# GpSimd issues the output projection's stores, norms come in one transfer, head sums are split sooner, x is added late to two rows

## The chip, the cores and the metric

The kernel runs on one core of a Trainium2 chip. The metric is device time in microseconds (us) of one execution. Before the change it is 1361.49 us, the median of three runs (1359.12 to 1362.36).

## The reference

A decoder layer in float32, one batch of 2048 positions, width 1024. The input x is RMS-normalised and projected to 6144 columns. These feed a gated short convolution of 8 heads of 128 and a linear recurrent unit (LRU) of 16 heads of 64. Each head's output is RMS-normalised, multiplied by its gain and a SiLU gate; the 2048 columns go through one output projection, x is added, and a last RMS norm follows.

```
xn = rms_norm(x, ln_g)
proj = xn @ w_in                                   # 1024 -> 6144
y_conv = headwise_rms_norm(short_conv(...), 8, conv_out_g) * silu(g_conv)
y_lru = headwise_rms_norm(rg_lru(...), 16, lru_out_g) * silu(g_lru)
h = x + concat([y_conv, y_lru]) @ w_out            # 2048 -> 1024
out = rms_norm(h, final_g)
```

## The kernel before

**Products.** A float32 product is made of three matmuls of rounded operands: each operand is split into a high half (ScalarE's cast) and a low half (a subtraction on VectorE, DVE, or GpSimd), and high x high, high x low and low x high are summed in PSUM. Blocks of 1024 x 1024 are multiplied with seven instead of eight products of halves. The tiles `th`, `tl` hold the split half that stays for many steps (the right side), `s` the split half of one step (high and low side by side).

**Steps.** A step makes the products for one pair of row blocks or columns. `steps` lists 48 steps of the input projection and then 16 of the output projection, ("o", ph, m): ph = 0 is the LRU half of the 2048 columns, ph = 1 the convolution half, and m names rows 2m and 2m + 1 of 16 blocks of 128 positions. A step has six to eight slots, and a slot is 12 matmuls of 128 x 512 on one bank (line 924). The first step of a ph "opens" new right-side tiles, which `Change` loads and splits (lines 492, 435, 163).

**The order** is written by hand. `at(n, f)` puts f n slots later; `tick()`, called once a slot, runs what is due. Each engine takes its instructions strictly in the order in which they are written, and SyncE (SP), which issues nearly all DMAs, too: a DMA that waits for an engine holds up all behind it.

**Left side of the output projection.** The gated outputs, not yet normalised, lie in DRAM (`yd`, stored at line 624), and the reciprocal roots of the heads' mean squares in `rsd`. `load_z` loads two row blocks of `yd` into `raw` (line 292) and the norms, broadcast over partitions, into `zr`, and multiplies them on DVE (line 163). For ph = 1 the norm of one head serves 128 partitions, one transfer (line 282). For ph = 0 heads are 64 wide, so a tile needs two norms, in two transfers of 64 partitions (line 285). Steps m = 0 and 1 of both ph are made during the input projection (`jobs`, the preparation): their `s` tiles are stored in `so` and only loaded later. Steps m = 2 to 7 of ph = 0 load their rows two steps ahead.

**Head norms.** `finish` multiplies by the gate, stores, squares; `head_sums` reduces the squares of each head group on DVE (line 609). After the last one `head_norms(1)` runs: one slot later the sums are split (`rt`: a cast, line 575, and a subtraction on DVE), three slots after that TensorE sums them over partitions (`norm_ps`, line 582), then a transpose, a root, a reciprocal (line 603) and twelve stores of eight partitions each into `rsd` (line 595). These norms serve the rows from m = 4 on.

**Rows of the output.** In ph = 0, `outp` loads x (line 847), adds the products and stores the partial sum to `od` (line 857); in ph = 1 it loads `od`, adds, takes the mean square on ScalarE (line 863), scales on DVE (line 868) and stores the finished row (line 872). All these DMAs are SP's. The last step ends with a shorter path of its own (lines 877 to 887).

Of the kernel before, what the change touches and what calls it, by code (L numbers as in the profile page):

```python
# [15 lines left out]
ALU = mybir.AluOpType  # L16

P = 128
D = 1024
# [4 lines left out]
KT = D // P  # L24
# [14 lines left out]
def hymba_kernel(ctx: ExitStack, tc: tile.TileContext, x, xt, w_in, par, lamc, w_gate, w_out, final_g, out):  # L39
    nc = tc.nc  # L40
# [103 lines left out]
    def at(slots, *fs):  # L144
        if slots == 0:
            for f in fs:
                f()
        else:
            due.append([slots, fs])
# [105 lines left out]
    steps = [(kind, 0, k) for k in range(KT) for kind in "lab"]  # L255
    steps += [(kind, 1, k) for kind, k in zip("lablab", (0, 1, 1, 1, 0, 0))]
    steps += [(kind, 1, k) for k in range(2, KT) for kind in "lab"]
    steps += [("o", ph, m) for ph in range(2) for m in range(KT)]
    cols = {"l": (GLX, GLG), "a": (GC, GX), "b": (GB, GG)}

    def set_of(n):
# [7 lines left out]
    def load_z(h, m, zr, wait):  # L269
        r = [piece("raw") for _ in range(4)]  # L270
        fs = []
        for i in range(2):
            c, b = divmod(2 * m + i, NB)
            assert normed[c // 2]
            rs_ = rsd[c // 2][c % 2]
            zz_, zq_ = [], []
            z2 = wt(("u", "r")[i], "zr") if zr else None

            def norms(dst, k0, n):
                dst = dst.rearrange("p (k t) -> p k t", k=n)  # L280
                if h == 1:
                    nc.sync.dma_start(dst, rs_[b:b + 1, k0:k0 + n, :].broadcast_to((P, n, P)))
                else:
                    for w in range(2):
                        nc.sync.dma_start(dst[w * 64:w * 64 + 64], rs_[b:b + 1, k0 + w * KT:k0 + w * KT + n, :]
                                          .broadcast_to((64, n, P)))

            for q in range(2):
                zz = r[2 * i + q].rearrange("p (k t) -> p k t", k=NB)
                zq = z2[:, q * C:(q + 1) * C] if zr else piece("zr")  # L290
                k0 = (1 - h) * KT + q * NB
                nc.sync.dma_start(zz, yd[c][b, :, k0:k0 + NB, :])
                if not zr:
                    norms(zq, k0, NB)
                elif q == 1:
                    norms(z2, (1 - h) * KT, KT)
                zq = zq.rearrange("p (k t) -> p k t", k=NB)
                fs.append(lambda zz=zz, zq=zq: tt(zz, zz, zq, ALU.mult))
        if wait is not None:
            for i in range(2):  # L300
                at(max(wait + i, 1), *fs[2 * i:2 * i + 2])
        return r, fs
# [19 lines left out]
    def hl_done(n):  # L322
        hlc[0] -= n
# [15 lines left out]

    def jobs():  # L340
        tjobs = [(t, j) for t in (2, 3) for j in range(NB)]
        for ph, m in ((0, 0), (0, 1), (1, 0), (1, 1)):
            (a11, a12, a21, a22), fs = load_z(ph, m, False, None)
            yield from (None,) * 4
            for f in fs[:2]:
                f()
            yield
            for f in fs[2:]:
                f()
            yield  # L350
            if m:
                x_ = aux("s3")
                tt(x_, a11, a21, ALU.subtract)
                tt(a21, a21, a22, ALU.add)
            b = {}

            def blocks():
                if tjobs:
                    b[0] = tjobs.pop(0)
                    b[1] = [piece("traw") for _ in range(4)]  # L360
                    for p, src in zip(b[1], w_blocks(*b[0])):
                        nc.sync.dma_start(p, src)

            def sums():
                if b:
                    b11, b12, b21, b22 = b[1]
                    tt(b11, b12, b11, ALU.subtract)
                    tt(b12, b22, b12, ALU.subtract)

            def more():  # L370
                if b:
                    b11, b12, b21, b22 = b[1]
                    tt(b22, b22, b11, ALU.subtract)
                    tt(b21, b21, b22, ALU.subtract)
                    to = td[b[0]]
                    at(1, lambda: [nc.sync.dma_start(to[n], v) for n, v in enumerate((b22, b11, b12, b21))])
                    b.clear()

            blocks()
            prev = None  # L380
            nothing = lambda: None
            if m:
                items = [(0, a11, lambda: tt(a11, a21, a11, ALU.subtract)), (3, x_, nothing), (2, a21, nothing),
                         (1, a11, nothing), (4, a12, lambda: tt(a12, a12, a11, ALU.subtract)),
                         (6, a22, nothing), (5, a12, nothing)]
            else:
                items = [(n, v, nothing) for n, v in enumerate((a12, a22, a11, a21))]
            for n, (i, v, after) in enumerate(items):
                if prev:
                    prev()  # L390
                    prev = None
                while not may():
                    yield
                t, = hl_tile("so")
                nc.scalar.copy(t[:, 0:C], v)

                def prev(t=t, i=i, v=v, after=after, dst=so[ph, m]):
                    tt(t[:, C:2 * C], v, t[:, 0:C].bitcast(F32), ALU.subtract)
                    after()
                    at(2, lambda: nc.sync.dma_start(  # L400
                        dst[i], t.bitcast(F32).rearrange("p (h c) -> p h c", h=2)))
                    at(3, lambda: hl_done(1))

                yield
            prev()
            made.add((ph, m))
            sums()
            yield
            more()
            yield  # L410
            yield
            blocks()
            yield from (None,) * 4
            sums()
            yield
            more()
            yield from (None,) * 2
# [149 lines left out]
    def head_norms(h):  # L567
        sm_ = sums[0]
        rt, = hl_tile("rt")
        rh, rl = rt[:, 0:C], rt[:, C:2 * C]  # L570
        at(6, lambda: hl_done(1))
        v = {}

        def split():
            nc.scalar.copy(rh, sm_)
            tt(rl, sm_, rh.bitcast(F32), ALU.subtract)

        def add():
            v["ps"] = pss.tile([P, C], F32, tag="s", name="norm_ps")[:NR, 0:KT * R]
            parts = [(n, q) for n in range(2) for q in (rh, rl)]  # L580
            for m, (n, q) in enumerate(parts):
                nc.tensor.matmul(v["ps"], sel[n], q[:, (1 - n) * KT * R:(2 - n) * KT * R],
                                 start=m == 0, stop=m == 3)

        def root():
            v["rs"] = aux("hn")[:NR, 0:KT * R]
            nc.vector.transpose(v["rs"], v["ps"])
            nc.scalar.activation(out=v["rs"], in_=v["rs"], func=AF.Sqrt, scale=inv_hd, bias=eps[:NR])

        def store():  # L590
            for w in range(3):
                k0 = (w + 1) % 3 * KT
                for q in range(4):
                    p0 = w * R + q * 8
                    nc.sync.dma_start(
                        rsd[h].rearrange("i b k t -> (i b) k t")[:, k0:k0 + KT, q * R:(q + 1) * R],
                        v["rs"][p0:p0 + 8].rearrange("p (k r) -> p k r", k=KT))
            normed[h] = True

        split()  # L600
        at(3, add)
        at(4, root)
        at(5, lambda: nc.vector.reciprocal(out=v["rs"], in_=v["rs"]))
        at(5, store)

    def head_sums(h, kt, y):
        if summed[0] == 0:
# [4 lines left out]
        summed[0] += 1  # L612
        if summed[0] == 2 * KT:
            summed[0] = 0
            at(1 if h else 7, lambda: head_norms(h))

    def finish(d0, h, kt, y, sil, gain):
        def f1():
# [191 lines left out]
    def conv_b(h, k):  # L810
        g = wt("o2", "gb", bufs=O2)

        def put(which, bank, other):
# [12 lines left out]
                combine(g[:, 0:C] if which == 21 else g[:, C:N2], bank, other)  # L826
            if which == 21:
                silu(g)
                finish(6, h, k, t, g, pt[:, CG + k:CG + k + 1])

        return put

# [4 lines left out]
    def outp(ph, m):  # L837
        ob = [wt("hl", "ob", bufs=HL) for _ in range(2)]
        xr, rest = {}, []
        if ph == 1 and m == 0:  # L840
            fg[0] = wt("t", "fg")
            nc.sync.dma_start(fg[0], final_g.rearrange("(o d) -> o d", o=1).broadcast_to((P, D)))

# [2 lines left out]
            xr[i] = wt("ig", "xr", bufs=IG) if i == 0 else wt("o2", "xr", bufs=O2)  # L846
            nc.sync.dma_start(xr[i], x[tb * P:(tb + 1) * P, :] if ph == 0 else od[tb])

        last = ph == 1 and m == KT - 1
        at(2 if last else 5, lambda: load(0))  # L850
        at(2 if last else 6, lambda: load(1))

        def fin(i):
            tb = 2 * m + i
            if ph == 0:
                at(1, lambda: tt(xr[i], xr[i], ob[i], ALU.add))
                at(3, lambda: nc.sync.dma_start(od[tb], xr[i]))
                return
            ss = small.tile([P, 2], F32, tag="ss", bufs=4, name="ss")
            rs = small.tile([P, 1], F32, tag="rs", bufs=4, name="rs")  # L860
# [8 lines left out]
                                               op0=ALU.mult, op1=ALU.mult)  # L869

            def f3():
                nc.sync.dma_start(out[tb * P:(tb + 1) * P, :], ob[i])

            if last and i == 1:
                for d in (1, 0):
# [419 lines left out]
```

## Time and profile before

| | us |
|---|---|
| median of three runs | 1361.49 |
| the profiled execution | 1361.65 |
| its span (first to last instruction) | 1359.8 |
| TensorE (PE) busy | 1301.9, 96% |
| DVE busy | 1032.5, 76% |
| ScalarE (ACT) busy | 748.4, 55% |
| GpSimd (POOL) busy | 226.2, 17% |
| SP's DMA queue, share of 16 engines | 77.1% |

The output projection runs from about 1025 us to the end. The profile's page has the busy times; its windows give, for a stretch of the span, the busy us and instruction count of each engine, the granted TensorE clock (1.00 is full), the share of the 16 DMA engines' time that packets took, and GB/s. The share can pass 1.00, since packets of one engine overlap. A row of the waits names who waited for whom, us in total, times, and the longest. A row of a timeline has start, duration, engine, line and names, and in brackets the idle time before it with what ended it.

### The profile page before, as it was taken

The numbers are of one execution on the slowest core, as the hardware profiler recorded it, in microseconds if no ns is written. First come the engines' busy times: TensorE is split into PE (matmuls) and PEld (weight loads), VectorE is DVE, ScalarE is ACT, GpSimd is POOL, SyncE is SP. The second block draws the span as 40 slices with busy tenths as digits, with TensorE's granted clock in tenths as the row PEclk, the third lists the DMA queues.
The fourth block names the chain that finished last, engine by engine and source line by source line (L and its number), as shares of the span: only waits on it lengthen the run. The fifth ranks groups of instructions, "written<-read, shape, count | busy, mean of one in ns | idle before, by whom it ended". The sixth has DMA issues, their size and how long they took to land.

```text
span 1359.8 us, 16618 instructions
## 1 busy us (share of the span) xinstructions
PE 1301.9 (96%) x5648; PEld 1058.6 (78%) x5648; DVE 1032.5 (76%) x1245; ACT 748.4 (55%) x1139; POOL 226.2 (17%) x160
## 2 busy tenths in 40 slices
PE   6989999999999999899999999999999799998997
PEld 5867877777878787777888888888878688887886
DVE  7778788789989897978566676667458776759885
ACT  7475757575665757565544645364456233444443
POOL 3204242333334340101010110101000000000000
PEclk9989999999999999999999999999999899999999
DMA  7137797988879888542789999999778889797643
GB/s 284 31 119 258 270 252 273 278 296 302 319 281 330 291 291 304 173 162 79 247 304 286 335 354 331 332 339 365 228 253 313 249 236 227 271 404 260 240 146 136
DMA packets 158805, 355.28 MB, mean 261 GB/s; under 512 B 17920, under 2 KB 52736, under 8 KB 158720
## 3 DMA queue, kind: packets, MB, share of 16 engines
q1 hardware_dynamic: 158432, 353.90, 77.1%
q8 instruction: 45, 0.74, 0.2%
q14 instruction: 40, 0.33, 0.1%
q10 hardware_dynamic: 288, 0.32, 0.1%
HBM read 217.11 MB, written 137.04 MB: 260 GB/s over the span
## 4 chain that ended last, share of the span: by engine, by line
PE 40%; DMA 7%; DVE 4%; ACT 3%; issue 1%; SPq 0%; DVEq 0%; ACTq 0%
PE bank L924 40%; DMA traw<-td 1%; DMA zr<-rsd 1%; PE gate L704 1%; ACT i L711 1%; ACT r L711 1%; DVE tl L163 1%; DMA traw<-in_w_out_dram 1%; DMA od<-xr 1%; DMA xr<-od 1%; DVE s L163 1%; DMA xr<-in_x_dram 1%; ACT th L435 1%; DMA yd<-gl 0%; DMA raw<-yd 0%
## 5 line engine op out<-in xcount | busy, mean ns | idle before, releaser
L924 PE MATMUL bank<-th,s 128*128 128x512 f32 x3632 | 1138.8, 392 | 19.9 <-ACT u L1232 10.0
L924 PEld LDWEIGHTS bank<-th,s 128*128 128x128 f32 x3632 | 686.1, 189 | 173.5 <-ACT u L1232 15.0
L924 PE MATMUL bank<-tl,s 128*128 128x512 f32 x1816 | 711.1, 392 | 1.6 <-DVE tl L163 1.3
L924 PEld LDWEIGHTS bank<-tl,s 128*128 128x128 f32 x1816 | 343.2, 189 | 74.8 <-DVE tl L163 3.5
L163 POOL TENSOR_TENSOR s<-raw,s 128x512 fp32r<-128x512 f32 x62 | 110.2, 1790 | 253.9 <-ACT s L200 210.7
L200 ACT CAST s<-raw 128x512 fp32r<-128x512 f32 x140 | 84.5, 616 | 75.4 <-PE bank L924 41.8
L163 DVE TENSOR_TENSOR tl<-traw,th 128x512 fp32r<-128x512 f32 x117 | 85.1, 763 | 40.4 <-ACT th L435 30.0
L1232 ACT COPY u<-bank 128x512 f32<-128x512 f32 x58 | 34.0, 586 | 145.6 <-PE bank L924 77.8
L163 DVE TENSOR_TENSOR s<-s,s 128x512 fp32r<-128x512 f32 x105 | 95.5, 909 | 10.5 <-ACT s L200 10.5
L163 POOL TENSOR_TENSOR gb<-gb,sg 128x1024 f32<-128x1024 f32 x16 | 40.6, 2537 | 348.3 <-ACT sg L637 328.2
L163 DVE TENSOR_TENSOR s<-raw,s 128x512 fp32r<-128x512 f32 (+1 forms) x125 | 92.7, 765 | 6.5 <-ACT s L982 4.4
L200 ACT CAST s<-s 128x512 fp32r<-128x512 f32 x105 | 64.7, 616 | 30.3 <-DVE s L163 25.8
L435 ACT CAST th<-traw 128x512 fp32r<-128x512 f32 x96 | 55.1, 618 | 30.7 <-DMA traw<-td 17.8
L1229 ACT COPY q<-bank 128x512 f32<-128x512 f32 x58 | 33.9, 584 | 68.0 <-PE bank L924 59.2
L678 DVE SCALAR_TENSOR_TENSOR u<-xl,pt,u 128x1024 f32<-128x1024 f32 x48 | 62.7, 1306 | 6.3 <-ACT u L674 5.7
L163 DVE TENSOR_TENSOR raw<-raw,zr 128x512 f32<-128x512 f32 x64 | 41.2, 684 | 34.6 <-DMA zr<-rsd 31.1
L1235 ACT COPY rr<-bank 128x512 f32<-128x512 f32 x58 | 33.8, 583 | 50.4 <-PE bank L924 50.4
L788 DVE SCALAR_TENSOR_TENSOR t<-p,pt,t 128x1024 f32<-128x1024 f32 x32 | 46.5, 1454 | 5.9 <-ACT t L785 5.1
L163 DVE TENSOR_TENSOR st<-u,st 64x1024 fp32r<-64x1024 f32 x32 | 46.5, 1452 | 1.0
L711 ACT ACTIVATE r<-gate,pt 64x512 f32<-64x512 f32 x64 | 43.8, 684 | 3.1 <-PE gate L704 2.4
L163 POOL TENSOR_TENSOR gl<-gl,sg 128x1024 f32<-128x1024 f32 x16 | 40.4, 2523 | 24.5 <-ACT sg L637 24.5
L711 ACT ACTIVATE i<-gate,pt 64x512 f32<-64x512 f32 x64 | 43.8, 684 | 1.1
(153 smaller groups left out, 1153.7 us busy)
## 6 DMA issues: line engine op xcount, KB each, us to landing
sd<-s SPq DMA_DIRECT2D x151, 512.0 KB
s<-sd SPq DMA_DIRECT2D x151, 512.0 KB
raw<-in_w_in_dram SPq DMA_DIRECT2D x104, 256.0 KB
raw<-yd SPq DMA_DIRECT2D x64, 256.0 KB
traw<-in_w_out_dram SPq DMA_DIRECT2D x64, 256.0 KB
so<-so SPq DMA_DIRECT2D x22, 512.0 KB
s<-so SPq DMA_DIRECT2D x22, 512.0 KB
yd<-gl SPq DMA_DIRECT2D x32, 256.0 KB
```

The costliest lines, as they stand in the source:

```text
L163: (eng or nc.vector).tensor_tensor(out=out, in0=a, in1=b, op=op)
L200: nc.scalar.copy(dst[i][0], val(i))
L435: nc.scalar.copy(self.dst[i, j][0], self.r[i, j])
L678: nc.vector.scalar_tensor_tensor(out=v["u"], in0=o1[:, 1 + j:1 + j + N2], scalar=lw[j], in1=v["u"], op0=ALU.mult, op1=ALU.add)
L704: nc.tensor.matmul(ps[j], v["gw"][n][:, j, :], v["st"][j][:, sl], start=(n == 0), stop=(n == 1))
L711: nc.scalar.activation(out=g_[hi, sl], in_=v["ps"][j][src], func=AF.Sigmoid, bias=pt[src, bias + k:bias + k + 1])
L788: nc.vector.scalar_tensor_tensor(out=tcur["t"], in0=p[:, 2 + j:2 + j + N2], scalar=cw[j], in1=tcur["t"], op0=ALU.mult, op1=ALU.add)
L924: nc.tensor.matmul(bank, a[:, js], b, start=start and n == 0, stop=stop and n == 2, skip_group_check=more)
L1229: nc.scalar.copy(q1, bk["A"])
L1232: nc.scalar.copy(u2, bk["A"])
L1235: nc.scalar.copy(rr, bk["A"])
```

## The change

Five edits, none of which changes what is computed.

1. Stores of partial sums (`od`) and of finished rows, but for the last step's, are issued by GpSimd instead of SP.
2. For ph = 0, the two transfers of norms for 64 partitions each become one, whose source has the shape (2, 64, n, 128) with a step of 0 over the 64.
3. The last two steps of the input projection finish one slot sooner, and the split of the head sums follows the last reduction in the same slot; matmul, root and stores stay two slots later relative to it, so in the same slots as before.
4. The steps m = 0 and 1 no longer load and add x in ph = 0, but store the bare products; in ph = 1 they load and add x as well as the partial sum.
5. In ph = 1 these two steps come last (m = 2, 3, 4, 5, 6, 7, 0, 1), and the preparation makes m = 2 and 3 of ph = 1 instead of 0 and 1.

```
-    steps += [("o", ph, m) for ph in range(2) for m in range(KT)]
+    steps += [("o", 0, m) for m in range(KT)]
+    steps += [("o", 1, m) for m in (2, 3, 4, 5, 6, 7, 0, 1)]
+    X_LATE = (0, 1)
...
                 if h == 1:
                     nc.sync.dma_start(dst, rs_[b:b + 1, k0:k0 + n, :].broadcast_to((P, n, P)))
                 else:
-                    for w in range(2):
-                        nc.sync.dma_start(dst[w * 64:w * 64 + 64], rs_[b:b + 1, k0 + w * KT:k0 + w * KT + n, :]
-                                          .broadcast_to((64, n, P)))
+                    src = rs_[b].rearrange("(w k) t -> w k t", k=KT)[1:3, k0 - KT:k0 - KT + n, :]
+                    nc.sync.dma_start(dst, src.unsqueeze(1).broadcast_to((2, 64, n, P)))
...
-        for ph, m in ((0, 0), (0, 1), (1, 0), (1, 1)):
+        for ph, m in ((0, 0), (0, 1), (1, 2), (1, 3)):
...
-        at(6, lambda: hl_done(1))
+        d = 2 if h else 0
+        at(6 + d, lambda: hl_done(1))
...
         split()
-        at(3, add)
-        at(4, root)
-        at(5, lambda: nc.vector.reciprocal(out=v["rs"], in_=v["rs"]))
-        at(5, store)
+        at(3 + d, add)
+        at(4 + d, root)
+        at(5 + d, lambda: nc.vector.reciprocal(out=v["rs"], in_=v["rs"]))
+        at(5 + d, store)
...
-            at(1 if h else 7, lambda: head_norms(h))
+            at(0 if h else 7, lambda: head_norms(h))
...
-                finish(6, h, k, t, g, pt[:, CG + k:CG + k + 1])
+                finish(5 if h and k == KT - 1 else 6, h, k, t, g, pt[:, CG + k:CG + k + 1])
...
-        last = ph == 1 and m == KT - 1
-        at(2 if last else 5, lambda: load(0))
-        at(2 if last else 6, lambda: load(1))
+        def row(i):
+            xo = wt("o1", "xo", n=N2 + 4)[:, 0:D]
+            tb = 2 * m + i
+            nc.sync.dma_start(xo, x[tb * P:(tb + 1) * P, :])
+            return lambda: tt(xr[i], xr[i], xo, ALU.add)
+
+        def rows(first, i):
+            load(i)
+            first.append(row(i))
+
+        last = ph == 1 and m == 1
+        if ph == 1 and m in X_LATE:
+            add = []
+            order = (1, 0) if last else (0, 1)
+            at(1, lambda: rows(add, order[0]))
+            at(2, lambda: load(order[1]))
+            at(3 if last else 4, lambda: (add[0](), add.append(row(order[1]))))
+            at(5 if last else 7, lambda: add[1]())
+        elif ph == 1 or m not in X_LATE:
+            at(5, lambda: load(0))
+            at(6, lambda: load(1))
...
+            if ph == 0 and m in X_LATE:
+                at(2, lambda: nc.gpsimd.dma_start(od[tb], ob[i]))
+                return
             if ph == 0:
                 at(1, lambda: tt(xr[i], xr[i], ob[i], ALU.add))
-                at(3, lambda: nc.sync.dma_start(od[tb], xr[i]))
+                at(3, lambda: nc.gpsimd.dma_start(od[tb], xr[i]))
                 return
...
-                nc.sync.dma_start(out[tb * P:(tb + 1) * P, :], ob[i])
+                (nc.sync if last else nc.gpsimd).dma_start(out[tb * P:(tb + 1) * P, :], ob[i])
```

What this moves on the engines, in the order of their instructions. First DVE, around the last reduction of head sums; before:

```order
787 L163 TENSOR_TENSOR tl<-traw,th 128x512 x4
788 L609 TENSOR_REDUCE sums<-t 128x32
789 L163 TENSOR_TENSOR raw<-raw,zr 128x512 x2
790 L163 TENSOR_TENSOR xr<-xr,ob 128x1024
791 L163 TENSOR_TENSOR tl<-traw,th 128x512 x2
792 L163 TENSOR_TENSOR raw<-raw,zr 128x512 x2
793 L163 TENSOR_TENSOR rt<-sums,rt 128x512
```

On DVE at the same place, after (`rt` is the split of the sums, `raw<-raw,zr` the products with the norms of step m = 2, `xr<-xr,ob` the addition of x):

```order
784 L163 TENSOR_TENSOR tl<-traw,th 128x512 x6
785 L611 TENSOR_REDUCE sums<-t 128x32
786 L163 TENSOR_TENSOR rt<-sums,rt 128x512
787 L163 TENSOR_TENSOR tl<-traw,th 128x512 x2
788 L163 TENSOR_TENSOR raw<-raw,zr 128x512 x2
789 L163 TENSOR_TENSOR tl<-traw,th 128x512 x2
790 L163 TENSOR_TENSOR raw<-raw,zr 128x512 x2
791 L163 TENSOR_TENSOR s_8788<-raw 128x512
```

The split now follows the reduction at once, ahead of both products with norms, and the addition of x between them is gone.

Second, SP's queue where the rows of m = 2 and 3 are loaded; before:

```order
448 L285 DMA zr<-rsd_88 64x1024 x2
449 L292 DMA raw<-yd_85 128x512 x2
450 L285 DMA zr<-rsd_88 64x1024 x2
451 L226 DMA s<-so_119 128x1024
452 L624 DMA yd_86<-gb 128x4x128
453 L624 DMA yd_87<-gb 128x4x128
454 L857 DMA od_134<-xr 128x1024
455 L226 DMA s<-so_119 128x1024
456 L857 DMA od_135<-xr 128x1024
457 L292 DMA raw<-yd_85 128x512 x2
458 L285 DMA zr<-rsd_88 64x1024 x2
```

On SP after (`zr<-rsd` are the norms, `s<-so` the prepared tiles of m = 1, `yd<-gb` the last gated outputs):

```order
446 L287 DMA zr<-rsd_88 128x1x1024
447 L293 DMA raw<-yd_85 128x512 x2
448 L287 DMA zr<-rsd_88 128x1x1024
449 L626 DMA yd_86<-gb 128x4x128
450 L626 DMA yd_87<-gb 128x4x128
451 L226 DMA s<-so_119 128x1024 x2
452 L293 DMA raw<-yd_85 128x512 x2
453 L287 DMA zr<-rsd_88 128x1x1024
```

Each pair of broadcasts is one, the stores to `od` have left the queue, and the last gated outputs stand ahead of both loads of prepared tiles.

Third, SP's queue where the second half's first rows finish; before:

```order
538 L282 DMA zr<-rsd_88 128x1024
539 L292 DMA raw<-yd_85 128x512 x2
540 L282 DMA zr<-rsd_88 128x1024
541 L226 DMA s<-so_123 128x1024 x2
542 L872 DMA out_dram<-ob 128x1024
543 L292 DMA raw<-yd_85 128x512 x2
```

On SP at that place after (`out_dram<-ob` is the finished row):

```order
512 L284 DMA zr<-rsd_89 128x1024
513 L293 DMA raw<-yd_86 128x512 x2
514 L284 DMA zr<-rsd_89 128x1024
515 L226 DMA s<-so_125 128x1024 x2
516 L293 DMA raw<-yd_86 128x512 x2
517 L284 DMA zr<-rsd_89 128x1024
```

The finished row no longer stands between the prepared tiles and the next step's loads; it is on GpSimd's queue, behind its last multiplication and the stores to `od`.

More of the change, by code (lines that the diff above doesn't have):

```diff
@@ L350, in jobs @@
             yield
-            if m:
+            if m % 2:
                 x_ = aux("s3")
@@ L381, in jobs @@
             nothing = lambda: None
-            if m:
+            if m % 2:
                 items = [(0, a11, lambda: tt(a11, a21, a11, ALU.subtract)), (3, x_, nothing), (2, a21, nothing),
@@ L839, in outp @@
         xr, rest = {}, []
-        if ph == 1 and m == 0:
+        if ph == 1 and m == 2:
             fg[0] = wt("t", "fg")
```

## The prediction

> **What bounds the kernel now.** I read the page first, then who waits for whom on TensorE after 1000 us, then the timelines around the two stretches where it stands, then the DMA views. The page:
>
> ```profile
> span 1359.8 us, 16618 instructions
> ...
> PE 1301.9 (96%) x5648; PEld 1058.6 (78%) x5648; DVE 1032.5 (76%) x1245; ACT 748.4 (55%) x1139; POOL 226.2 (17%) x160
> ```
>
> The profiled execution took 1361.65 us, 1.9 us more than its span and 0.16 us from the median of 1361.49; sums below start at 1361.65. TensorE is the bound, so a gain can only come out of its idle 4%, and of that the change touches the output projection, from about 1025 us on. There, TensorE's waits are:
>
> ```profile
> PE norm_ps L582 <- DVE rt L163: 7.1, 1, 7.1
> PE bank L924 <- ACT u L1232: 3.8, 1, 3.8
> ```
>
> Two stretches hold nearly all of it. The windows give PE's busy time and matmuls, further on its clock, the DMA share and GB/s; the first row is a stretch without a wait.
>
> ```profile
> 1100.00:1150.00 50.00, 50.00 (x222) 41.27 (x221) 35.36 (x52) 16.14 (x28) 0.00 (x0) 1.00 0.86 216
> ...
> 1055.00:1075.00 20.00, 12.89 (x49) 10.27 (x48) 11.41 (x19) 5.84 (x9) 0.00 (x0) 0.74 1.05 297
> 1225.00:1240.00 15.00, 10.95 (x41) 8.24 (x40) 12.59 (x20) 5.25 (x10) 0.00 (x0) 0.89 0.83 289
> ```
>
> At 222 matmuls in 50 us, one takes 0.225 us. 1055 to 1075 should hold 89 and holds 49, four of them of half width, so 47: 42 missing, 9.4 us. 1225 to 1240 should hold 66.6 and holds 41: 5.8 us. More than the waits themselves, since the granted clock is down (0.74, 0.89) after each. So 15 us is the most that the change can win.
>
> Why the first gap: TensorE's matmul of the norms, and DVE (start, duration, line, names, idle before).
>
> ```profile
> 1064.53 0.95 PE L582 MATMUL norm_ps<-rt,sel 128*96 128x256 f32 x3 [7.11 <-DVE rt L163]
> ...
> 1051.49 1.26 DVE L609 TRANSPOSE_TENSOR_REDUCE sums<-t 128x32 f32<-128x1024 f32 x1
> 1058.12 1.29 DVE L163 TENSOR_TENSOR raw<-raw,zr 128x512 f32<-128x512 f32 x2 [5.38 <-DMA zr<-rsd]
> 1059.34 1.22 DVE L163 TENSOR_TENSOR xr<-xr,ob 128x1024 f32<-128x1024 f32 x1
> 1060.47 1.29 DVE L163 TENSOR_TENSOR tl<-traw,th 128x512 fp32r<-128x512 f32 x2
> 1062.58 1.29 DVE L163 TENSOR_TENSOR raw<-raw,zr 128x512 f32<-128x512 f32 x2 [0.82 <-DMA zr<-rsd]
> 1063.79 0.68 DVE L163 TENSOR_TENSOR rt<-sums,rt 128x512 fp32r<-128x512 f32 x1
> ```
>
> The sums are ready at 1052.75, but their split, rt, which the norm matmul needs, stands in DVE's order behind products that wait for norms (zr) to land. So a late load holds up work that doesn't use it.
>
> **The change part by part.** *Sums split sooner.* The same split and matmuls, no new instruction. By the order it now follows the last reduction, so it would end near 1053.5, ahead of 1057.4, where TensorE began to wait: the 7.1 us go. What is late next is the load itself: the tiles of the first step that isn't prepared (m = 2). TensorE would want its first low half three short norm matmuls and 24 full ones later, 0.3 + 5.4 us, at 1063.1. The second pair of norms lands at 1062.6 today, and products, sums, one combination and the subtraction on DVE (1.3 + 1.4 + 0.7 + 0.7, each from the like row) bring it to 1066.7 without the split in between. So by this edit alone 3.6 us of the gap stay, with some loss of clock.
>
> *x left out of two rows until the end.* Two steps of the first half no longer load x (four loads of 512 KB) nor add it; the last two steps do both. DVE's work is equal: four additions of 1.22 us move. At 407 GB/s (the 1200 row below) the two loads ahead of m = 2's norms are worth 2.6 us of its landing. In the last steps there is room:
>
> ```profile
> 1340.00:1350.00 10.00, 10.00 (x46) 8.29 (x45) 4.56 (x7) 1.64 (x5) 0.00 (x0) 1.00 0.23 91
> ```
>
> DVE is half idle and the DMA three quarters, and in the last step the second addition falls three slots (3 x 12 matmuls, 8 us) before the last bank. I take nothing; without that cover it costs an addition, 1.2 us, and at most the idle time of a late load, like DVE's 5.4 above.
>
> *Stores from GpSimd.* SP's queue is in order, so loads stood behind stores that waited for DVE. Between 1190 and 1260 us the longest such wait is (total, times, longest):
>
> ```profile
> SPq L872 <- DVE ob L868: 11.4, 4, 7.0
> ```
>
> The 7.0 is SP standing at the first finished row, with the next step's loads behind it; they may go up to 7 us sooner. But the second gap begins with loads that are already under way, and DVE's chain after them, so I count 0 to 3 us of its 5.8 and take 1.5. GpSimd computes nothing there (its column is 0.00 in every window above), so 30 issues there hide: no row prices one, SP's take 0.3 us, and at 5 us each they would fill half of 310 us. A store waiting on GpSimd has only stores behind it. Their bytes share the same 16 engines, and two of them (1 MB, 2.6 us) now come before m = 2's norms: that may take back what the x loads gave.
>
> *Norms in one transfer.* In the half that reads LRU norms, two broadcasts of 64 rows become one whose source is (2, 64, n, 128): 12 of 512 KB in the projection and, in two bursts of four, 8 of 256 KB in the preparation. Its price depends on how many of the 16 DMA engines it runs on. The nearest row is the only transfer of the kernel with an outer size under 16, the eight-row stores of norms.
>
> ```profile
> DMA packets 158805, 355.28 MB, mean 261 GB/s; under 512 B 17920, under 2 KB 52736, under 8 KB 158720
> ...
> sd<-s SPq DMA_DIRECT2D x151, 512.0 KB
> ...
> rsd<-hn SPq DMA_DIRECT2D x24, 8.0 KB
> ...
> pt<-in_par_dram ACTq DMA_DIRECT2D x1, 52.0 KB
> rsx<-rs SPq DMA_DIRECT2D x2, 2.0 KB
> lam<-in_lam_dram SPq DMA_DIRECT2D x1, 4.0 KB
> ```
>
> The list of issues, first and last shown, sums to 956. Of the 17,920 packets under 512 B, data are 24 x 64 (rsd, runs of 128 B), 2 x 512 (rsx, single elements) and 128 each of pt and lam: 2,816. The other 15,104 are completions. Sixteen for each issue would be 15,296; 192 are missing, which is 24 x 8. So an eight-row store runs on eight engines: the outer size sets how many take part. Whether a source of outer size 2 against a tile of 128 rows gets 2 or 16, no row says; these are the two ends. I take 2, since the only row under 16 follows the outer size, and I assume that an engine's share is cut along the outer step of both sides. The Trainium skill (DMA: Bandwidth & Descriptors, on why a DMA increments its semaphore by 16) has a rule for it: the number of engines is the largest, up to 16, that divides the slowest dimension of both sides; by that rule it would be 2. The eight-row stores agree with the rule; both their sides are eight, so they don't test it on unlike sides.
>
> What 2 would cost comes from rows of the windows and of SP's and DVE's timelines:
>
> ```profile
> 1200.00:1215.00 15.00, 15.00 (x67) 12.40 (x67) 5.53 (x8) 7.05 (x13) 0.00 (x0) 1.00 1.04 407
> ...
> 1050.00:1100.00 50.00, 42.26 (x176) 33.95 (x175) 33.60 (x51) 16.94 (x29) 0.00 (x0) 0.90 0.91 259
> ...
> 1048.55 1.09 SPq L285 DMA_DIRECT2D zr<-rsd  x2
> ...
> 1154.19 1.29 DVE L163 TENSOR_TENSOR raw<-raw,zr 128x512 f32<-128x512 f32 x2 [1.40 <-DMA zr<-rsd]
> ```
>
> Full DMA moves 407 GB/s, 25.4 per engine. 256 KB on each of two engines is 10.3 us, against 1.3 us on sixteen. Twelve are 124 us. The remaining traffic from 1048.6 to 1154.2: (259 + 216) GB/s x 50 us + about 1.3 MB for the last 5 us = 25 MB, less 6.3 MB of norms and 1 MB of x, 17.7 MB, 43 us. Those two engines need 167 us where 106 were used: 61 us more, 58 with the x loads ahead of it gone. The loads of the second half, behind in the same queue, already fill the DMA (1.04), so nothing is caught up later. The two PE gaps vanish in this wait. In the preparation, a burst of four costs 4 x (5.2 - 0.6) = 18 us on those engines.
>
> ```profile
> L285 SPq DMA_DIRECT2D zr<-rsd x40: 444/463/1143, 661.0 to 1143.6; - x40
> ...
> 666.42 1.08 SPq L285 DMA_DIRECT2D zr<-rsd  x2
> ...
> 680.90 1.26 DVE L163 TENSOR_TENSOR raw<-raw,zr 128x512 f32<-128x512 f32 x2
> ```
>
> Of the 40 half-broadcasts, 24 are the projection's and 16 these. DVE takes the last pair of the first burst 13.4 us after its issue, so part is covered; between 0 and 18 per burst I take 8, 16 for both. Sum: 1361.65 + 58 + 16 = 1435.6, say 1435. Its own range is 1400 (20 us of the lead regained, preparation hidden) to 1470 (preparation in full, and clock lost after stalls).
>
> **The rivals.** *Faster: the merged load stays on 16 engines.* Then the sum is the other edits': first gap, 9.4 us, of which 3.6 stay, less 0 to 2.6 for x, plus clock and the next load: I keep 3; second gap -1.5. 1361.65 - 6.4 - 1.5 = 1353.7, range 1349 to 1360. For it: the tile side has 128 rows, and the 64-row and 128-row broadcasts show all sixteen completions. Against: the eight-row row. The Trainium skill (same page, rules for kernel authors) also speaks for it: two transfers to disjoint partition halves gain nothing, one of 128 partitions should replace them. By that sentence alone the merge is harmless; no run here shows it with such a source.
>
> *No change: the load is the wall.* Still 16 engines, but stores sent early from GpSimd push m = 2's norms back by their 2.6 us, and the second gap stays; TensorE waits for s where it waited for rt. 1358 to 1365. The saturated DMA (1.05 in 1055 to 1075) speaks for it; against it that x is as much as the stores.
>
> *A little slower, by GpSimd alone:* its stores land so late that ob and xr buffers stall the next steps. It decides once a store takes over a step (84 matmuls, 19 us) longer than now. 1366 to 1375. GpSimd's idleness speaks against it.
>
> **How the numbers follow.** Two engines 0.55, sixteen and faster 0.36, no change 0.06, GpSimd's stall 0.03. The first isn't higher since the decisive size, 2 against 128, has no row. 0.3% (4.1 us) is about what a measurement of this kernel can tell from none: faster 0.36, same 0.06, slower 0.58. The predicted time is the first case's, 1435. From 1350 to 1460 lie about 0.29 of the faster case, the 0.09 of the two between, and 0.45 of the first: 0.83. Its width comes from two signs, not from doubt within one; the likeliest case's own range is 1400 to 1470.
>
> **What would show it.** Right: 40 broadcasts of 16 completions become 20 of 2, so the packets under 512 B fall by 600 (by 320 if each has 16; GpSimd's own completions aside); DVE idles ten us and more for zr in each step of the first half, TensorE behind it, with GB/s well under 216 there. Also rt follows the reduction and norm_ps no longer waits, whatever the total. Wrong: DVE's waits for zr at 3 to 5 us as now, and the total under 1361.

## The result and the profile after

The changed kernel takes 1461.26 us (median of 4, 1456.72 to 1462.60), the kernel before beside it 1360.30 us (median of 4, 1357.68 to 1362.36): a ratio of 1.0742, 95% interval 1.0722 to 1.0761, so 101 us slower. Its profiled execution took 1460.77 us, with a span 99.2 us longer than before. The page after:

```profile
span 1459.0 us, 16628 instructions
...
PE 1318.8 (90%) x5648; PEld 1070.3 (73%) x5648; DVE 1032.9 (71%) x1245; ACT 748.6 (51%) x1139; POOL 244.0 (17%) x190
...
DMA packets 158206, 355.28 MB, mean 244 GB/s; under 512 B 17320, under 2 KB 52136, under 8 KB 158120
```

The bytes are those of before and the small packets 17,920 - 17,320 = 600 fewer: exactly 40 broadcasts with 16 completions each (640) against 20 with two (40). TensorE has the same 5648 matmuls, but takes 16.9 us longer for them and idles 82.3 us more. What DVE waits for, before:

```profile
DVE raw L163 <- DMA zr<-rsd: 31.1, 11, 5.4
```

and after:

```profile
DVE raw L163 <- DMA zr<-rsd: 118.9, 16, 14.2
```

Whom TensorE waits for in the whole span, before (with norm_ps, 7.1, in the prediction):

```profile
PE bank L924 <- ACT u L1232: 10.0, 10, 3.8
```

and after:

```profile
PE bank L947 <- ACT u L1255: 63.9, 15, 21.7
PE bank L947 <- DMA s<-sd: 26.2, 2, 15.4
```

Most of the waits for ScalarE's `u` (55.8 of 63.9 us, from 1060 to 1300) are for a bank of the output projection that is emptied late. ScalarE in turn waits for DVE, which stands at its products with late norms; from 1075 to 1260 us after:

```profile
ACT u L1255 <- DVE ob L163: 56.8, 5, 12.7
```

The two waits for `s<-sd` lie in the preparation, in the input projection. In a window of the first half of the output projection (before, 1100 to 1150 had 222 matmuls and 216 GB/s; columns as there):

```profile
1100.00:1150.00 50.00, 28.41 (x102) 22.47 (x103) 18.87 (x29) 11.50 (x19) 1.06 (x2) 0.75 0.36 120
```

And one of several stretches of 5 us there whose traffic is no more than one load of norms moves:

```profile
1145.00:1150.00 5.00, 5.00 (x24) 4.14 (x23) 0.00 (x0) 1.21 (x2) 0.00 (x0) 1.00 0.13 52
```

0.13 is two sixteenths, 52 GB/s two engines at 26: fourteen engines stand still while two carry 512 KB. In windows of 1 us, the share is below 0.12 in only four from 1076 to 1253 us (0.05 to 0.07 from 1133 to 1136, 0.10 at 1187). So the two engines hardly ever pause in this stretch.

Where the 99.2 us lie can be read from the first issue and the last product of these loads in the projection, 1048.55 and 1154.19 before. After, on SP and on DVE:

```profile
1075.84 0.51 SPq L287 DMA_DIRECT2D zr<-rsd  x1
```

```profile
1253.31 1.29 DVE L163 TENSOR_TENSOR raw<-raw,zr 128x512 f32<-128x512 f32 x2 [10.76 <-DMA zr<-rsd]
```

The first comes 27.3 us later, although the first burst of the preparation began 2.6 us sooner (658.4 us after, 661.0 before): 29.9 us are lost in the preparation. The stretch grows from 105.6 to 177.5 us: 71.9 in the projection. 29.9 - 2.6 + 71.9 = 99.2, the whole difference of the spans, and nothing is caught up behind it. In the preparation, before:

```profile
655.00:705.00 50.00, 50.00 (x222) 41.37 (x221) 30.17 (x34) 22.58 (x30) 5.89 (x4) 1.00 0.90 306
...
745.00:800.00 55.00, 54.78 (x241) 44.76 (x240) 39.50 (x46) 28.44 (x39) 5.91 (x4) 1.00 0.94 331
```

and after, two bursts of four merged loads in these stretches:

```profile
655.00:705.00 50.00, 38.31 (x159) 30.90 (x158) 22.76 (x24) 17.19 (x22) 2.79 (x2) 0.90 0.62 200
...
745.00:800.00 55.00, 39.43 (x165) 31.75 (x164) 22.24 (x27) 15.43 (x22) 5.88 (x4) 0.84 0.71 232
```

63 and 76 matmuls are missing, 139 x 0.225 = 31 us, near the 29.9. The loads of TensorE's next `s` stand behind each burst on SP's queue. TensorE gets its `s` late after the first burst:

```profile
687.38 0.77 PE L947 MATMUL bank<-th,s 128*128 128x512 f32 x1 [10.88 <-DMA s<-sd]
```

The sooner split does what the change says: rt follows the reduction, and no norm matmul waits. On DVE after:

```profile
1075.63 1.25 DVE L611 TRANSPOSE_TENSOR_REDUCE sums<-t 128x32 f32<-128x1024 f32 x1
1077.54 0.69 DVE L163 TENSOR_TENSOR rt<-sums,rt 128x512 fp32r<-128x512 f32 x1 [0.65 <-ACT rt L577]
```

### The profile page after: what moved, and what is told of

It reads as the page before. It is cut to its first block, busy times and chain, and to the rows that moved or that the text cites. A ratio compares the mean times of both kernels' runs of the same rounds, so it can differ in the third digit from the quotient of the medians.

```text
span 1459.0 us, 16628 instructions
## 1 busy us (share of the span) xinstructions
PE 1318.8 (90%) x5648; PEld 1070.3 (73%) x5648; DVE 1032.9 (71%) x1245; ACT 748.6 (51%) x1139; POOL 244.0 (17%) x190
## 2 busy tenths in 40 slices
DMA packets 158206, 355.28 MB, mean 244 GB/s; under 512 B 17320, under 2 KB 52136, under 8 KB 158120
## 4 chain that ended last, share of the span: by engine, by line
PE 43%; DMA 21%; DVE 16%; ACT 6%; issue 5%; SPq 1%; POOL 0%; DVEq 0%; ACTq 0%; POOLq 0%
PE bank L947 41%; DMA zr<-rsd 11%; DVE s L163 4%; DMA sd<-s 2%; DMA yd<-gl 2%; PE gate L706 1%; ACT i L713 1%; ACT r L713 1%; DVE tl L163 1%; DMA raw<-in_w_in_dram 1%; DVE u L680 1%; DMA s<-sd 1%; DMA s<-so 1%; DVE sums L611 1%; DMA xcol<-in_xt_dram 1%
## 5 line engine op out<-in xcount | busy, mean ns | idle before, releaser
L947 PE MATMUL bank<-th,s 128*128 128x512 f32 x3632 | 1152.5, 396 | 110.0 <-ACT u L1255 63.9
L947 PEld LDWEIGHTS bank<-th,s 128*128 128x128 f32 x3632 | 694.2, 191 | 268.8 <-ACT u L1255 70.8
L947 PEld LDWEIGHTS bank<-tl,s 128*128 128x128 f32 x1816 | 347.4, 191 | 75.6 <-DVE tl L163 2.8
L163 DVE TENSOR_TENSOR tl<-traw,th 128x512 fp32r<-128x512 f32 x117 | 83.6, 750 | 39.7 <-ACT th L436 29.1
```

Of the source, the lines that this page charges most:

```text
L163: (eng or nc.vector).tensor_tensor(out=out, in0=a, in1=b, op=op)
L947: nc.tensor.matmul(bank, a[:, js], b, start=start and n == 0, stop=stop and n == 2, skip_group_check=more)
```

## The experiments

The theory after the result: a merged load runs on as many engines as its source's outer size says, two, and these two engines are the limit; the other four edits are harmless. Rivals: the other edits cause the loss; or a merged load is slow for another reason (its size, its place in SP's order). All ratios are to the kernel before, run on the same chip.

| kernel | median, us | ratio | 95% interval |
|---|---|---|---|
| the change | 1461.26 | 1.0742 | 1.0722 to 1.0761 |
| merge_alone | 1472.99 | 1.0844 | 1.0823 to 1.0865 |
| merge_prep | 1390.63 | 1.0236 | 1.0219 to 1.0253 |
| merge_proj | 1438.34 | 1.0592 | 1.0570 to 1.0615 |
| no_merge | 1351.83 | 0.9959 | 0.9943 to 0.9974 |
| copies2 | 1391.99 | 1.0245 | 1.0225 to 1.0265 |
| copies8 | 1355.71 | 0.9980 | 0.9969 to 0.9992 |
| merge_nox | 1442.59 | 1.0626 | 1.0610 to 1.0642 |
| after_first | 1456.47 | 1.0728 | 1.0712 to 1.0744 |
| no_merge_first | 1350.62 | 0.9948 | 0.9931 to 0.9966 |
| gp_alone | 1354.74 | 0.9978 | 0.9964 to 0.9992 |
| split_alone | 1359.12 | 1.0004 | 0.9993 to 1.0015 |
| xlate_alone | 1355.29 | 0.9979 | 0.9964 to 0.9993 |

**Which edit.** Kernel merge_alone has only this edit on the kernel before; merge_prep has it under `if n == NB` (the preparation's size), merge_proj under `if n == KT` (the projection's).

```diff
-                    for w in range(2):
-                        nc.sync.dma_start(dst[w * 64:w * 64 + 64], rs_[b:b + 1, k0 + w * KT:k0 + w * KT + n, :]
-                                          .broadcast_to((64, n, P)))
+                    src = rs_[b].rearrange("(w k) t -> w k t", k=KT)[1:3, k0 - KT:k0 - KT + n, :]
+                    nc.sync.dma_start(dst, src.unsqueeze(1).broadcast_to((2, 64, n, P)))
```

> The kernel before with one edit only, the norms of two heads in one transfer. If that transfer runs on two DMA engines and is the whole loss: 1360 + 28 for the preparation (TensorE's delay after its two bursts in the trace of the changed kernel) + 73 to 82 for the projection (delay from there to the last step with such norms, with and without the gap that the sooner split won back) = 1461 to 1470; packets under 512 B at 17320, norm_ps still waits for the split and longer than 7.1 us, since the late load stands before it. If instead GpSimd's stores, the later x or the new order cause the loss: at most 1375.

> The kernel before with merged norms only in the preparation (8 transfers of 256 KB in two bursts), the projection as before. Two engines by the trace after: 1360 + 28 = 1388 (1380 to 1395), and the projection keeps its period and its 7.1 us wait of norm_ps. As the prediction put it (18 us per burst, 8 uncovered): 1360 + 16 = 1376. If a burst is hidden behind other work: 1360 to 1364.

> The kernel before with merged norms only in the projection (12 transfers of 512 KB), the preparation as before. Two engines by the trace after: 1360 + 73 to 82 = 1433 to 1442. As the prediction put it: 1360 + 58 = 1418. If the two places add up, the excesses of this run and of the run with the preparation alone make that of the run with both.

Measured against the 1357.8 beside them: 115 us for the edit alone, 32.8 in the preparation, 80.5 in the projection. 32.8 + 80.5 = 113.3, so the two places add up, and the edit alone is more than the whole loss; merge_alone is 3 us above what was expected. The preparation costs twice the 16 of the prediction, the projection more than its 58.

merge_alone loses 14 us more (the ratios' difference, 0.0102 x 1359) than the whole change, though without the merge the other edits save only 6 (no_merge below). A part of this can be read in SP's waits of merge_alone from 1100 to 1260 us:

```profile
SPq L856 <- DVE xr L163: 46.1, 3, 15.7
```

L856 is the store to `od`, still on SP there. It waits for DVE's addition of x, which waits behind DVE's product with the late norms, and the next norms stand behind it in SP's queue. SP, then DVE, of merge_alone:

```profile
1174.17 1.22 SPq L285 DMA_DIRECT2D zr<-rsd  x1
...
1201.89 0.32 SPq L856 DMA_DIRECT2D od<-xr  x1
...
1203.57 0.51 SPq L285 DMA_DIRECT2D zr<-rsd  x1
```

```profile
1166.35 1.29 DVE L163 TENSOR_TENSOR raw<-raw,zr 128x512 f32<-128x512 f32 x2 [8.72 <-DMA zr<-rsd]
...
1198.23 1.29 DVE L163 TENSOR_TENSOR raw<-raw,zr 128x512 f32<-128x512 f32 x2 [8.72 <-DMA zr<-rsd]
```

The last load of a step is used at 1198.23, and the next is issued at 1203.57: 5.3 us without norms under way in a step of 31.9 us, while the changed kernel, with the stores on GpSimd, makes a step in 28.7 us (below). In most of the 5.3 us the engines still carry other loads; the DMA share is 0.00 only from 1201.5 to 1202.5 us, so this explains a part of the 3.2 us per step. So GpSimd's stores seem worth more where loads are late; this is read from the traces, not tried apart.

Kernel no_merge is the changed kernel with the two transfers back, the diff above reversed.

> The changed kernel with the two transfers of 64 partitions put back, so the other four edits alone. If the merged transfer is the whole loss: the prediction's faster rival, 1353.7 (1349 to 1360), no wait of norm_ps for the split, PE's wait before the bank of m = 2 at most 3.6 us. If GpSimd's stores, the later x or the new order cause the loss: 1440 or more, about as the changed kernel.

Measured 1351.83, 0.4% less than before, and near the prediction's rival of 1353.7 for unharmed loads. The rival "the other edits cause the loss" is out. In the trace of no_merge the stretch from the first issue to the last product with norms is 99.1 us (1044.09 to 1143.17). Against it the changed kernel's 177.5 is 78.4 longer, close to merge_proj's 80.5: the 71.9 found above is what is left after the gains of the other edits.

**How many engines.** Kernels copies2 and copies8 are the changed kernel, with the LRU norms kept in DRAM two and eight times (NCP), so that the merged load's source has an outer size of 4 and 16. The lines that load and copy:

```diff
-                    src = rs_[b].rearrange("(w k) t -> w k t", k=KT)[1:3, k0 - KT:k0 - KT + n, :]
-                    nc.sync.dma_start(dst, src.unsqueeze(1).broadcast_to((2, 64, n, P)))
+                    src = rsc[c // 2][c % 2][b].rearrange("w c k t -> (w c) k t")[:, k0 - KT:k0 - KT + n, :]
+                    nc.sync.dma_start(dst, src.unsqueeze(1).broadcast_to((2 * NCP, 64 // NCP, n, P)))
...
+            nc.gpsimd.dma_start(rsc[h].rearrange("i b w c k t -> (i b w) c (k t)"),
+                                rsl[h].rearrange("i b w k t -> (i b w) (k t)").unsqueeze(1)
+                                .broadcast_to((4 * NB, NCP, KT * P)))
```

> The changed kernel, the LRU norms stored twice in DRAM (one DRAM to DRAM copy on GpSimd's queue after the norms), so that the merged load's source is (4, 32, n, 128) instead of (2, 64, n, 128). If the source's outer size sets the number of engines: four, packets under 512 B some 40 more than with two (20 transfers with 4 completions instead of 2); a 512 KB load takes 5.2 us instead of 10.3, twelve take 62, with the other 20 MB (49 us) 111 us, near the 106 of before; the preparation's bursts 10.3 instead of 20.6 us. So about 1370 (1358 to 1385), far from 1461. If the merged transfer is slow for another reason (its size, its place in the queue, the shape of its source): 1450 or more.

> As the one with two copies, but with eight, the source (16, 8, n, 128). If the source's outer size sets the number of engines: all sixteen, 16 completions each, and the time of the kernel with two transfers and the other four edits, 1352 (1346 to 1356); lower than that if sixteen engines reading one and the same row of DRAM are slower than sixteen reading copies. If the merged transfer is slow for another reason: 1450 or more.

Measured 1391.99 and 1355.71. The packets, copies2:

```profile
DMA packets 158342, 355.55 MB, mean 256 GB/s; under 512 B 17392, under 2 KB 52208, under 8 KB 158256
```

and copies8:

```profile
DMA packets 158774, 356.33 MB, mean 264 GB/s; under 512 B 17632, under 2 KB 52448, under 8 KB 158688
```

Without the completions of the LRU norms' loads there would be 17,920 - 640 = 17,280. The changed kernel has 40 more: 20 loads with 2. copies2 has 112 more: 20 with 4, and 2 x 16 for the two copies (32 fits both kernels). copies8 has 352 more: 20 with 16, and 32. So the outer size of the source, 2, 4 or 16, against a tile of 128 rows sets the number of engines, and the loss goes with it: 101, 33 and -3 us. The rule that the prediction cited (the Trainium skill, DMA: Bandwidth & Descriptors, on why a DMA increments its semaphore by 16) agrees, here on unlike sides. A merged load as such isn't slow. Nor is it the reading of one row 64 times: no_merge's two transfers do that too. It isn't faster either: copies8, which also pays for its copies, is no better than no_merge with its two transfers, and a gain from reading copies of a row did not show.

copies2 missed: 1392 against 1370 (1358 to 1385). Its windows in the preparation, and from 1050 to 1150 us:

```profile
655.00:705.00 50.00, 45.48 (x194) 36.90 (x193) 26.50 (x30) 18.96 (x25) 5.90 (x4) 0.97 0.82 270
...
745.00:800.00 55.00, 46.73 (x199) 37.87 (x198) 32.22 (x38) 25.61 (x36) 3.48 (x3) 0.94 0.83 278
...
1050.00:1100.00 50.00, 36.19 (x150) 29.07 (x149) 27.28 (x40) 18.76 (x32) 1.15 (x2) 0.86 0.64 212
1100.00:1150.00 50.00, 43.57 (x176) 34.74 (x175) 28.11 (x44) 12.76 (x23) 3.19 (x6) 0.93 0.62 197
```

In the preparation 28 and 42 matmuls are missing against before, 16 us, half of the 31 us at two engines. From 1050 to 1150 TensorE lacks 118 of 444 matmuls (27 us), where before it lacked 46: 72 more, another 16 us. From the first issue to the last product with norms it is 126.7 us (1059.84 to 1186.56), while the sum of bytes is 62 us of norms and, at 203 GB/s less the norms, 48 us of other traffic, 110 in all. So in the projection, at four engines, the sum of bytes per engine no longer fills the time; waiting for one load is a candidate, but no run takes it apart, and it stays open.

**Engines or order of issue.** Two kernels on the changed one. merge_nox doesn't load x in the first half and so leaves it out of twelve row blocks of the output; after_first issues a row block's norms ahead of its raw loads.

```diff
-            nc.sync.dma_start(xr[i], x[tb * P:(tb + 1) * P, :] if ph == 0 else od[tb])
+            if ph == 1:
+                nc.sync.dma_start(xr[i], od[tb])
...
-                at(1, lambda: tt(xr[i], xr[i], ob[i], ALU.add))
+                at(1, lambda: tt(xr[i], ob[i], ob[i], ALU.add))
```

```diff
+            if zr:
+                norms(z2, (1 - h) * KT, KT)
             for q in range(2):
...
-                elif q == 1:
-                    norms(z2, (1 - h) * KT, KT)
```

> The changed kernel without the twelve loads of x in the first half of the projection; DVE's additions stay (they add the products to themselves), so x is left out of twelve rows of blocks and DVE's work is the same. If the two engines' throughput sets the step (20.6 us of norms and a sixteenth each of the other 3 MB, 28.3 us by that sum, 28.8 in the trace): 1 MB less per step is 2.6 us less, the step 26.2 us, the whole 13 to 16 us under the changed kernel's 1461, so 1445 to 1448. If the order in which SP issues the loads sets it: no change, within 4 us of 1461.

> The changed kernel with the norms of a row issued ahead of its two raw loads, which wait for their buffers (SP waits 56 us there, 11 times, between 1100 and 1260 us). If the two engines' throughput sets the step: within 5 us of 1461. If the late issue sets it: up to 6.5 us per step sooner, so 1425 to 1440.

merge_nox: 0.0116 lower in its ratio, 15.8 us (1442.59 us). after_first: 0.0014 lower, 1.9 us (1456.47). DVE's products with norms, the second row of one step and of the next; the changed kernel:

```profile
1194.38 1.29 DVE L163 TENSOR_TENSOR raw<-raw,zr 128x512 f32<-128x512 f32 x2 [8.91 <-DMA zr<-rsd]
...
1223.07 1.29 DVE L163 TENSOR_TENSOR raw<-raw,zr 128x512 f32<-128x512 f32 x2 [9.05 <-DMA zr<-rsd]
```

and merge_nox:

```profile
1188.83 1.29 DVE L163 TENSOR_TENSOR raw<-raw,zr 128x512 f32<-128x512 f32 x2 [8.30 <-DMA zr<-rsd]
...
1214.45 1.29 DVE L163 TENSOR_TENSOR raw<-raw,zr 128x512 f32<-128x512 f32 x2 [8.42 <-DMA zr<-rsd]
```

The step is 28.7 us with 3 MB of other traffic and 25.6 with 2: 20.6 us of norms and 2.6 for each other MB (28.3 and 25.8 by that sum). In after_first DVE waits for something else instead:

```profile
DVE raw L163 <- DMA raw<-yd: 99.3, 13, 14.2
```

The raw loads are now issued last, behind the norms, and the step stays at 28.5 to 29.1 us (products at 1162.26, 1191.39 and 1219.90). The two engines' throughput is the limit, not SP's order.

no_merge_first makes the same change of order to no_merge:

> The four other edits with two transfers of norms, these issued ahead of the raw loads. DVE still waits 17.6 us for norms there; if part of that is late issue, 1 to 4 us less than 1351.8; if it is only the load's own time, the same within 1.5 us.

1350.62 us, ratio 0.9948 against 0.9959: within the intervals, no difference. These two are the fastest kernels of the study.

**The other edits one by one**, each on the kernel before. gp_alone has only GpSimd's stores (first diff), split_alone only the sooner split (second, with the `d = 2 if h else 0` of the change); xlate_alone is no_merge without these two.

```diff
-                at(3, lambda: nc.sync.dma_start(od[tb], xr[i]))
+                at(3, lambda: nc.gpsimd.dma_start(od[tb], xr[i]))
...
-                nc.sync.dma_start(out[tb * P:(tb + 1) * P, :], ob[i])
+                (nc.sync if last else nc.gpsimd).dma_start(out[tb * P:(tb + 1) * P, :], ob[i])
```

```diff
-            at(1 if h else 7, lambda: head_norms(h))
+            at(0 if h else 7, lambda: head_norms(h))
...
-                finish(6, h, k, t, g, pt[:, CG + k:CG + k + 1])
+                finish(5 if h and k == KT - 1 else 6, h, k, t, g, pt[:, CG + k:CG + k + 1])
```

> The kernel before with only the stores of partial sums and finished rows moved to GpSimd. As the prediction put it: 1.5 us less than before (0 to 3), out of the second gap; DVE's or SP's wait at the first finished row (7.0 us) gone. If the stores now collide with the loads they stood behind: 1 to 4 us more than before.

> The kernel before with only the head sums split sooner. As the prediction put it: the 7.1 us wait of norm_ps goes and 3.6 us of the first gap of 9.4 stay as a wait for the load of m = 2, so 3.5 to 6 us less than before. If the load is the wall: TensorE waits for s of m = 2 what it waited for the split, and the time is that of before within 2 us.

> The kernel before with x left out of two rows until the end and the new order of the second half, nothing else. As the prediction put it: 0 to 2.6 us less than before. With GpSimd's stores at 3.0 less and the sooner split at nothing, the rest of the 6.0 of all four would be 3.0, if they add up.

Measured: -3.0 us, +0.5 and -2.9 (ratio less 1, times 1359), each within about 2 us by its interval. They add up to -5.4, and no_merge has -5.6. Where each acts is seen in the matmuls of two windows around the two gaps (x after PE's time; 222 and 111 would be full). Before:

```profile
1050.00:1100.00 50.00, 42.26 (x176) 33.95 (x175) 33.60 (x51) 16.94 (x29) 0.00 (x0) 0.90 0.91 259
...
1215.00:1240.00 25.00, 20.95 (x85) 16.52 (x84) 18.34 (x29) 10.39 (x20) 0.00 (x0) 0.93 0.89 323
```

gp_alone:

```profile
1050.00:1100.00 50.00, 43.16 (x179) 34.86 (x178) 38.10 (x56) 16.12 (x27) 2.66 (x5) 0.90 0.91 264
...
1215.00:1240.00 25.00, 23.10 (x101) 18.58 (x101) 24.57 (x40) 13.28 (x25) 1.59 (x3) 1.00 0.82 279
```

split_alone:

```profile
1050.00:1100.00 50.00, 43.88 (x173) 35.33 (x174) 35.82 (x53) 16.59 (x28) 0.00 (x0) 0.90 0.85 243
```

xlate_alone:

```profile
1050.00:1100.00 50.00, 45.13 (x188) 36.37 (x187) 34.47 (x53) 16.00 (x27) 0.00 (x0) 0.93 0.78 222
```

GpSimd's stores win 16 matmuls (3.6 us) in the second gap, the later x 12 (2.7 us) in the first, and the sooner split none. What TensorE waits for instead in split_alone, from 1000 us on:

```profile
PE bank L925 <- ACT u L1233: 4.8, 2, 3.6
PE bank L925 <- DVE ob L163: 3.7, 1, 3.7
PE bank L925 <- ACT q L1230: 3.0, 1, 3.0
```

The 7.1 us of norm_ps are gone, and 11.5 us stand in these three; before, norm_ps and `u` made 10.9 together. The wait for `ob` ends at 1070.95 us, when DVE gets to it behind a product with late norms:

```profile
1067.80 1.30 DVE L163 TENSOR_TENSOR raw<-raw,zr 128x512 f32<-128x512 f32 x2 [4.75 <-DMA zr<-rsd]
```

It is the third pair of products, so the first of m = 3, not of m = 2. A late load of norms is the wall there, much as that rival said; what ends the other two waits is not shown.

## Why the prediction was right or wrong

The direction and the cause were right: two engines, 600 small packets fewer, DVE and TensorE waiting for norms at a fraction of the bandwidth. The time, 1461.3, lies in that case's own range (1400 to 1470), 26 us above its 1435 and 1.3 above the overall range, which ended at 1460 and so left out the top of the likeliest case. Both large terms were too small, by 14 us each.

- **The preparation, 16 us: wrong.** The step that failed is "part is covered ... I take 8" of 18 per burst. It was read from the 13.4 us between a load's issue and its use on DVE. But those 13.4 us cover only DVE's use; TensorE's own `s` loads stand behind the burst and came late. Measured 30 us in the change, 33 alone. The upper end, 36, was nearly the value: there was next to no cover, and with four engines (copies2) the loss was half of it. That the DMA was 0.90 and 0.94 busy there before, with little room to catch up, fits this, but no run varies it.
- **The projection, 58 us: mechanism right, size too small; 71.9.** The forecast stretch was 167 less 3 for x, 164; measured 177.5. The 124 us of norms stood. The step that failed is the rest, 43 us of other traffic less 3: it took 53.5. More bytes explain at most 6 of the 13.5 us: the other traffic was taken as 17.7 MB; after, 149 GB/s x 177.5 us = 26.4 MB went through, so 20.1 MB without the norms, 49.3 us instead of 43. The window of that stretch after, and its list of issues:

```profile
1075.84:1253.31 177.47, 117.26 (x458) 93.34 (x456) 68.26 (x103) 37.58 (x64) 4.80 (x9) 0.84 0.43 149
...
xr<-in_x_dram SPq DMA_DIRECT2D x10, 512.0 KB
```

  The stretch before held ten loads of x too, though 1 MB was taken off for two that leave it. But of the ten after, four are issued behind the last load of norms, so they need not delay it:

```profile
1230.89 0.51 SPq L287 DMA_DIRECT2D zr<-rsd  x1
1231.50 9.16 SPq L849 DMA_DIRECT2D xr<-in_x_dram  x4
```

  The 3 us for the x loads ahead don't show. 124 + 49.3 = 173.3; the last 4 us are not placed, and 3 of them may be the pause from 1133 to 1136 us.
- **Both gaps vanish in this wait: right** for the total. The other four edits still matter: without them the loss is 14 us larger (merge_alone).
- **Sixteen engines and faster (1353.7): the total of the other edits was about right**, 1351.8 to 1355.7 (no_merge, copies8). Its parts weren't: the split was given most of it (9.4 less 3.6) and gives nothing: other waits of the same size take its place, one of them for a late load, the "no change" rival's argument. The later x gives 2.9 (0 to 2.6 forecast), GpSimd's stores 3.0 (1.5 forecast, 0 to 3). The sentence of the Trainium skill that spoke for the merge (DMA: Bandwidth & Descriptors, rules for kernel authors) did not hold for this source: the merge cost 115 us alone.
- **GpSimd's stall: wrong**, its stores gain.

## What to carry to other kernels

Before two transfers are made one, look at the outer size of the new source as well as of the target: here 2 against 128 rows left two of sixteen engines at work, and 512 KB took 10 us. The number of completions in a profile's packet counts tells how many engines worked. The time from a slow load's issue to its use says little about its cover: here the loads behind it were late, in a stretch whose DMA had been 0.9 busy. Taking away the wait that a profile names won nothing here, since other waits stood just behind it.

## What the runs showed of the hardware

An issue on SP can take long while two engines are backed up. In merge_alone, issuing one load of x:

```profile
1175.44 8.64 SPq L846 DMA_DIRECT2D xr<-in_x_dram  x1
```

8.64 us, where issues of x in the stretch before took 0.3 to 0.8 us each; all of SP's queue stands behind it, and the mean share of the 16 engines is 0.21 meanwhile. And waits have a second price: the same 5648 matmuls took 1301.9 us before, 1318.8 in the change and 1323.9 in merge_alone; the granted clock was 0.75 from 1100 to 1150 us in the change, and 1.00 before. GpSimd's issues, for which the trace of before had no price, take 0.53 us each (1.06 for two in the window above).
